# Weight sums of the feed-forward part planned one stage later, and lighter work around the first norm

## The chip, the cores and the metric

The kernel runs on one core of a Trainium2 chip. The metric is the device time of one execution in microseconds (us). The names of the engines are those of the profile: PE (matrix multiplication), PEld (its weight loads, which overlap it), DVE (vector), ACT (scalar), POOL (GpSimd) and SP, whose queue issues nearly all transfers (DMA). Every engine takes its instructions in the order in which they stand in its queue.

## The reference

One decoder layer is computed in float32 for 2048 prompt tokens and 64 sample tokens (8 sequences of 8) with shared weights, width 1024:

```python
hp = rmsnorm(xp, norm_mix_w[l])
mp, sr_p, sh_p = mixer(hp, pos_p, zero_ret, zero_hg, w_in[l], ...)
hs = rmsnorm(xs, norm_mix_w[l])
ms, sr_s, sh_s = mixer(hs, pos_s, state_ret[l], state_hgrn[l], w_in[l], ...)
xp = xp + mp
xs = xs + ms
hp = rmsnorm(xp, norm_ffn_w[l])
xp = xp + jnp.square(jax.nn.relu(hp @ w_up[l])) @ w_down[l]
hs = rmsnorm(xs, norm_ffn_w[l])
xs = xs + jnp.square(jax.nn.relu(hs @ w_up[l])) @ w_down[l]
```

The mixer projects to 4096 columns (`w_in`), runs four retention heads and four gated linear recurrences (HGRN2) over chunks, normalises each head, gates it, and projects back (`w_out`). The feed-forward part has 4096 inner columns. The outputs are the two normalised results and the final states of both recurrences.

## The kernel before

**Tiling and stages.** The tokens are cut in three groups: the first holds the 64 sample tokens and 512 of the prompt (576), the other two 768 prompt tokens each. The mixing part goes through them in turn: `mix` (four pairs of heads each) and then `out_proj`. In the profile `mix` of the first group lies at about 0 to 290 us, its `out_proj` up to 345, `mix` of the second group at 345 to 638, its `out_proj` up to 714, `mix` of the third group at 714 to 1010 and its `out_proj` up to 1076. Then come the three feed-forward stages, up to the end.

**A product.** A float32 product is made of three matmuls of rounded parts (high by high, high by low, low by high). So each weight block is loaded (`raw`), its high part cast on ACT (L310, into `hi`) and its low part subtracted on DVE (L318, into `lo`). Parts that were split before are loaded as they are (`hi<-fki0VA12hi`, `lo<-fki0VA12lo`). There are eight `raw` buffers and three `hi`/`lo` pairs. The two banks of `pj` take the products by turns, so a product that is two later than another has to wait until DVE has taken the earlier one out (L1035 and L1122 do that).

**Seven products for eight.** In the second and third group a pair of heads is computed with Strassen's scheme (Winograd's form) in two halves: a P part, seven products with L1848 (128x384 a matmul), and a V part, seven products with `product_t` (L1107, 128x256). Both take 84 ticks. The weights of four of the seven products are sums of weight blocks, named S1 to S4. For `w_in` these sums are made once, in the first group, by `in_sums` (DVE L417, stored by SP L424). For the feed-forward weights they are made ahead by `plan_sums`: a set has four loads of 512 KB (SP L1877), four sums on DVE (L1880, 128x1024) and four stores of 512 KB (SP L1885). There are 16 sets; a set's key is u0 to u7 or d00 to d31.

**What sets the order.** PE work counts ticks: `tick` is called after every two matmuls or so. `at` and `later` put a function on an agenda of ticks, `hold` puts one on a list of absolute ticks (`n_ticks`), and `plan_sums` has a queue of its own (`side`). A scheduler then puts each engine's instructions in an order; those inside `keep_in_program_order` stay as written.

**The first norm.** At the start `norm_in` rounds eight blocks of the input (ACT L715, DVE L716) while PE already multiplies them. The 64 sample columns of each high and low part are copied apart by POOL (L721, 16 copies, into `hs`). The squares (ACT L693) are added up on POOL and DVE by turns (L696), L774 adds the two halves, and PE sums the columns (L743). Two working buffers for the samples (`qm`) are cleared by POOL at L917. While the last heads of a group are computed, `norm_ahead` loads the next group's input a second time in eight quarters, squares each on ACT (L805) and adds it on DVE (L807).

**The last layers.** `out_proj` adds the residual on DVE (L246), and stores two results for the feed-forward part (`fres` and `fin`, SP L1912); `prepare` loads `fin` again (SP L1920).

Of the kernel before, what the change touches and what calls it, by code (L numbers as in the profile page):

```python
# [21 lines left out]
NS = NSEQ * SLEN  # L22
PAST = 16384
H = 4
# [28 lines left out]
NQ = FF // (4 * P)  # L53
# [152 lines left out]
class Kernel:  # L206
# [105 lines left out]
    def second_part(self, j):  # L312
        self.first_part(j)
        if j in self.second:
            hi, lo = self.wts[j]
            raw = self.second.pop(j)
            for c in (slice(0, WT),) if j else LEADS:
                self.nc.vector.tensor_tensor(out=lo[:, c], in0=raw[:, c], in1=hi.bitcast(F32)[:, c], op=ALU.subtract)  # L318
            if self.fast and j < N_IN:
                self.whole[j] = raw  # L320
                if j < 4:
                    if j >= 2:
                        self.hold((50, 74)[j - 2], self.in_sums, j)
                elif j % 4 >= 2:
                    self.in_sums(j)

# [166 lines left out]
    def build(self):  # L493
        nc, tc, I = self.nc, self.tc, self.I
        with ExitStack() as ctx:
# [84 lines left out]
            sums = [(("u", t), W_UQ0 + 4 * t) for t in range(NQ)]  # L580
# [2 lines left out]
            self.mix(gs[0])  # L583
            self.out_proj(gs[0], 1, lambda: norm(gs[1]))

            at = [84 * j if self.fast else 16 + 92 * j for j in range(2 * H)]
            self.plan_sums(sums[:NQ], at)
            self.mix(gs[1])
            self.out_proj(gs[1], 1, lambda: norm(gs[2]))
            self.plan_sums(sums[NQ:], at)  # L590
            self.mix(gs[2])

            def end_of_mixing():
# [105 lines left out]
    def norm_in(self, g, start=False, pace=5):  # L699


        nc, T = self.nc, g.T
        g.h, g.sq = [], None
        g.starts = ([0] if g.ns else []) + [g.ns + C * c for c in range(g.n // C)]

        def piece(kb):
            x, hi, lo = self.x_block(g, kb, start), self.getr(), self.getr()
            if start and kb == 0:
                raw = self.raws[0] = self.wp.tile([P, WT], F32, tag="raw", name="raw", bufs=self.n_raw)
                for c in LEADS:  # L710
                    self.fetch(raw[:, c], self.I["w"][0][:, c])
                self.ahead, self.w_load = 0, 1
                self.weight(0)
            w = self.vec[:, V_MIX + kb:V_MIX + kb + 1]
            nc.scalar.activation(hi[:, :T], x[:, :T], AF.Copy, scale=w)  # L715
            nc.vector.scalar_tensor_tensor(out=lo[:, :T], in0=x[:, :T], scalar=w, in1=hi.bitcast(F32)[:, :T],  # L716
                                           op0=ALU.mult, op1=ALU.subtract)
            if g.ns:

                for part, a in ((hi, 0), (lo, NS)):  # L720
                    nc.gpsimd.tensor_copy(self.hs[kb][:, a:a + NS], part[:, :NS])  # L721
            g.h.append((hi, lo))
            if start:
                g.x.append(x)
            else:
                g.sq = self.add_square(g, g.sq, x, nc.vector)

        def tables():
            cs = self.I["cs"].rearrange("p (a t) -> p a t", a=2)
            g.cos, g.sin = self.load(), self.load()  # L730
            self.fetch(g.cos[:, :T], cs[:, 0, g.off:g.off + T])
            self.fetch(g.sin[:, :T], cs[:, 1, g.off:g.off + T])

        def split():
            g.sq = self.halves(g, g.sq)

        def factor():
            g.rs, ln = self.get(), self.get()
            for hf, (c0, c1) in enumerate(g.pieces):
                sl = slice(c0, c1)  # L740
                ps = self.mm(c1 - c0)
                if start:
                    nc.tensor.matmul(ps, self.ones, g.sq[:, sl], start=True, stop=True)  # L743
                else:
                    self.column_sums(ps, *g.sq[hf])
                self.rsqrt(g.rs[:, sl], ps, ln[:, sl], self.eps, D)

        def factor_t():

            row = self.dp.tile([1, g.starts[-1] + C], F32, name=self.tag + f"r{g.i}")  # L750
            g.rt = self.small.tile([P, 8], F32, tag="rt", name="rt")
            nc.sync.dma_start(row, g.rs[0:1, :T])
            n0, m = g.ns, g.n // C
            with nc.allow_non_contiguous_dma("a column for each chunk"):
                nc.sync.dma_start(g.rt[:, len(g.starts) - m:len(g.starts)], row[0, n0:T].rearrange("(c p) -> p c", p=P))
                for a in range(0, P if n0 else 0, NS):
                    nc.sync.dma_start(g.rt[a:a + NS, 0:1], row[0, 0:NS].rearrange("(c p) -> p c", p=NS))

        def rotary():
            for t in (g.cos, g.sin):  # L760
                (nc.vector if self.fast else nc.gpsimd).tensor_tensor(out=t[:, :T], in0=t[:, :T], in1=g.rs[:, :T], op=ALU.mult)

        if start:
            g.x = []
            for kb in range(KB):
                piece(kb)
            part = [None, None]

            def square(kb):
                part[kb % 2] = self.add_square(g, part[kb % 2], g.x[kb], (nc.gpsimd, nc.vector)[kb % 2])  # L770

            def both():
                g.sq = part[0]
                nc.vector.tensor_tensor(out=g.sq[:, :T], in0=g.sq[:, :T], in1=part[1][:, :T], op=ALU.add)  # L774

            for kb in range(KB):
                self.at(24 + 2 * kb, square, kb)
            self.at(24 + 2 * KB, both)
        else:
            for kb in range(KB):  # L780
                self.later(pace * kb, piece, kb)
        t0 = 66 if start else pace * KB
        self.later(0 if start else t0, tables)
        if not start:
            self.later(t0 + 9, split)
        self.later(t0 + (0 if start else 20), factor)
        self.later(t0 + 24, rotary)
        self.later(t0 + 24, factor_t)

    def norm_ahead(self, g, early):  # L790


        nc, T, T2, n = self.nc, g.T, g.T // 2, g.n // C
# [37 lines left out]
            return  # L831
        todo = [(m, v, h) for h in range(2) for m in range(2) for v in range(2)]
        for k, a in enumerate(todo):
            self.later(1 + 9 * k, load, *a)
            self.later(12 + 9 * k, square, *a)
        for h in range(2):
            self.later(52 + 36 * h, split, h)
            self.later(60 + 36 * h, factor, h)
# [73 lines left out]
    def mix(self, g):  # L912
        nc = self.nc
        if g.ns:
            g.qm = [self.get(), self.get()]
            for q in g.qm:
                nc.gpsimd.memset(q, 0.0)  # L917
        g.o, g.oc = {}, {}
        end = 0
        for p in range(H):  # L920
# [1548 lines left out]
```

## Time and profile before

| What | Value |
|---|---|
| Median of 3 runs | 2384.07 us (2382.16 to 2389.36) |
| Profiled execution | 2385.9 us |
| Span in its profile | 2384.1 us |
| PE busy | 2353.4 us (99%) |
| DVE busy | 1800.1 us (76%) |
| ACT busy | 1229.9 us (52%) |
| POOL busy | 148.7 us (6%) |
| Data moved | 575.60 MB, 241 GB/s in the mean |

PE is busy for all but 30.7 us of the span. Each group of rows in the profile has a line, an engine, an operation, the tiles out<-in, a count and times; `PE pj L1107 <- DVE slab L1122` reads: PE's instruction of line 1107 that writes `pj` waited for what DVE wrote at line 1122. Rows of a time line start with the start time and the busy time of the group, and end with the idle time of the engine before it and what ended it. Rows by stretch give the stretch, its length, and the busy time and number of instructions of PE, PEld, DVE, ACT and POOL, then the TensorE clock that was granted (1.00 is full speed), the busy share of the DMA engines and GB/s.

### The profile page before, as it was taken

The numbers are of one execution on the slowest core, as the hardware profiler recorded it, in microseconds if no ns is written. First come the engines' busy times: TensorE is split into PE (matmuls) and PEld (weight loads), VectorE is DVE, ScalarE is ACT, GpSimd is POOL, SyncE is SP. The second block draws the span as 40 slices with busy tenths as digits, with TensorE's granted clock in tenths as the row PEclk, the third lists the DMA queues.
The fourth block names the chain that finished last, engine by engine and source line by source line (L and its number), as shares of the span: only waits on it lengthen the run. The fifth ranks groups of instructions, "written<-read, shape, count | busy, mean of one in ns | idle before, by whom it ended". The sixth has DMA issues, their size and how long they took to land.

```text
span 2384.1 us, 39317 instructions
## 1 busy us (share of the span) xinstructions
PE 2353.4 (99%) x15322; PEld 2313.5 (97%) x15322; DVE 1800.1 (76%) x2299; ACT 1229.9 (52%) x1974; POOL 148.7 (6%) x202
## 2 busy tenths in 40 slices
PE   9999999999999999999999999999999999999998
PEld 8888799999999999999999999999999999999997
DVE  7666777767676766757769997666998786669887
ACT  5555564466654555536555555444544364445444
POOL 4212201010001001000000000000000000000000
PEclk9999999999999999999999999999999999999999
DMA  8888788788858777968677665766755457575541
GB/s 284 288 295 285 253 282 311 280 287 288 315 199 308 289 285 267 322 218 294 227 244 268 234 214 183 241 212 223 243 185 191 152 188 262 201 237 178 203 152 71
DMA packets 232505, 575.60 MB, mean 241 GB/s; under 512 B 24179, under 2 KB 92659, under 8 KB 232310
## 3 DMA queue, kind: packets, MB, share of 16 engines
q1 hardware_dynamic: 232166, 572.98, 69.9%
q8 instruction: 122, 2.00, 0.3%
q14 instruction: 73, 0.60, 0.1%
q10 hardware_dynamic: 144, 0.02, 0.0%
HBM read 419.95 MB, written 151.66 MB: 240 GB/s over the span
## 4 chain that ended last, share of the span: by engine, by line
PE 81%; DVE 2%; DMA 1%; ACT 0%; issue 0%; POOL 0%; SPq 0%; DVEq 0%; ACTq 0%
PE pj L1848 34%; PE pf L1848 28%; PE pj L1107 9%; PE pj L452 6%; PE mm L1690 1%; PE mm L1688 1%; PE mm L1696 1%; PE mm L1618 0%; PE mm L1465 0%; PE mm L1376 0%; DMA lo<-fki0VA12lo 0%; PE mm L1837 0%; DMA raw<-w 0%; DMA fo<-slab 0%; DVE raw L1880 0%
## 5 line engine op out<-in xcount | busy, mean ns | idle before, releaser
L1848 PE MATMUL pj<-slab,hi 128*128 128x384 f32 (+1 forms) x3504 | 853.5, 326 | 1.4 <-ACT slab L1030 1.4
L310 ACT CAST hi<-raw 128x1024 fp32r<-128x1024 f32 (+1 forms) x449 | 470.6, 1049 | 676.0 <-PE pj L1848 258.9
L318 DVE TENSOR_TENSOR lo<-raw,hi 128x1024 fp32r<-128x1024 f32 (+1 forms) x449 | 551.8, 1229 | 165.9 <-ACT hi L310 147.1
L1848 PE MATMUL pf<-slab,hi 128*128 128x384 f32 (+1 forms) x2768 | 652.5, 321 | 0.0
L1848 PEld LDWEIGHTS pj<-slab,hi 128*128 128x128 f32 x3504 | 614.6, 188 | 1.7 <-ACT slab L1030 1.7
L1848 PE MATMUL pj<-slab,lo 128*128 128x384 f32 (+1 forms) x1752 | 570.6, 326 | 0.6 <-DVE lo L318 0.6
L1848 PEld LDWEIGHTS pf<-slab,hi 128*128 128x128 f32 x2768 | 480.6, 188 | 0.1
L1848 PE MATMUL pf<-slab,lo 128*128 128x384 f32 (+1 forms) x1384 | 443.1, 320 | 0.0
L1848 PEld LDWEIGHTS pj<-slab,lo 128*128 128x128 f32 x1752 | 329.3, 188 | 1.0 <-DVE lo L318 1.0
L1107 PE MATMUL pj<-hi,slab 128*128 128x256 f32 x1344 | 264.9, 290 | 6.9 <-DVE slab L1122 4.8
L452 PE MATMUL pj<-slab,hi 128*128 128x288 f32 (+1 forms) x1280 | 259.1, 318 | 2.0 <-ACT slab L715 1.1
L1848 PEld LDWEIGHTS pf<-slab,lo 128*128 128x128 f32 x1384 | 260.1, 188 | 0.0
L1107 PEld LDWEIGHTS pj<-hi,slab 128*128 128x128 f32 x1344 | 217.7, 193 | 8.3 <-ACT G L1439 5.1
L452 PEld LDWEIGHTS pj<-slab,hi 128*128 128x128 f32 x1280 | 206.5, 190 | 5.9 <-issue 1.9
L1107 PE MATMUL pj<-lo,slab 128*128 128x256 f32 x672 | 191.5, 285 | 0.8 <-DMA lo<-fki0VA12lo 0.8
L1940 ACT CAST slab<-slab 128x768 fp32r<-128x768 f32 (+1 forms) x192 | 145.5, 779 | 64.8 <-DVE slab L1951 47.3
L1944 DVE TENSOR_TENSOR slab<-slab 128x768 fp32r<-128x768 f32 (+1 forms) x192 | 167.3, 886 | 13.2 <-ACT slab L1940 4.6
L452 PE MATMUL pj<-slab,lo 128*128 128x288 f32 (+1 forms) x640 | 150.0, 315 | 0.0
L1107 PEld LDWEIGHTS pj<-lo,slab 128*128 128x128 f32 x672 | 130.1, 194 | 1.0 <-DMA lo<-fki0VA12lo 1.0
L452 PEld LDWEIGHTS pj<-slab,lo 128*128 128x128 f32 x640 | 108.6, 190 | 0.1
L2194 DVE TENSOR_TENSOR slab<-pf,slab 128x768 f32<-128x768 f32 (+1 forms) x87 | 76.5, 885 | 24.4 <-PE pf L1848 24.3
L2194 DVE TENSOR_TENSOR slab<-pj,slab 128x768 f32<-128x768 f32 (+1 forms) x79 | 70.1, 888 | 20.5 <-PE pj L1848 20.3
(269 smaller groups left out, 2614.4 us busy)
## 6 DMA issues: line engine op xcount, KB each, us to landing
raw<-w SPq DMA_DIRECT2D x255, 512.0 KB, 4.8
slab<-fu SPq DMA_DIRECT2D x64, 384.0 KB, 5.5
fu<-ld SPq DMA_DIRECT2D x60, 384.0 KB, 3.8
ld<-x SPq DMA_DIRECT2D x40, 384.0 KB, 5.5
ld<-fin SPq DMA_DIRECT2D x28, 384.0 KB, 4.8
slab<-fu SPq DMA_DIRECT2D x32, 288.0 KB, 4.5
fu<-ld SPq DMA_DIRECT2D x30, 288.0 KB, 3.2
fres<-slab SPq DMA_DIRECT2D x16, 384.0 KB, 4.6
```

Source lines behind the costliest of these rows:

```text
L310: self.nc.scalar.copy(self.wts[j][0][:, c], raw[:, c])
L318: self.nc.vector.tensor_tensor(out=lo[:, c], in0=raw[:, c], in1=hi.bitcast(F32)[:, c], op=ALU.subtract)
L452: self.nc.tensor.matmul(pj[:, i, :T2], w, a[:, c0:c1], start=j == 0 and q == 0, stop=j == n - 1 and q == 2)
L1107: self.nc.tensor.matmul(ps[:, tb * 256:(tb + 1) * 256], t, w[:, cols], start=first and kb == j == 0 and tb != 1, stop=kb == KB // 2 - 1 an ...
L1688: nc.tensor.matmul(dst, am(c), b["vc"][c][hd], start=True, stop=first)
L1690: nc.tensor.matmul(dst, qd[:, cols[c]], S, start=False, stop=True)
L1696: nc.tensor.matmul(ps[:, hd * P:(hd + 1) * P], kt[:, c * P:(c + 1) * P], b["vc"][c][hd], start=True, stop=True)
L1848: self.nc.tensor.matmul(*a, **k)
L1940: self.nc.scalar.copy(hi[:, :g.T], B[name][:, :g.T])
L1944: self.nc.vector.tensor_tensor(out=lo[:, :g.T], in0=B[name][:, :g.T], in1=hi.bitcast(F32)[:, :g.T], op=ALU.subtract)
L2194: nc.vector.tensor_tensor(out=r, in0=ps, in1=r, op=ALU.add)
```

## The change

Five places are edited, all on the path taken here (`self.fast`).

1. The sums of the first two weight pairs of `w_in` (`in_sums(2)`, `in_sums(3)`) are held until tick 78 and 94 instead of 50 and 74.
2. Each set of feed-forward sums starts 84 ticks later, which is one half of a pair of heads: the first P part of the second and of the third group has none. The second group makes seven sets instead of eight and the third nine, of which the last two start at tick 672 and 740 of the third group. Its `mix` has 8 x 84 = 672 ticks, so these two run in its `out_proj`.
3. The 16 copies of the sample columns are put on the agenda at tick 48 and on, one block a tick, instead of right behind each block.
4. `norm_ahead` loads and adds its quarters every 7 ticks instead of every 9: the last load at tick 50 instead of 64, the last square at 61 instead of 75.
5. The two clearings of `qm` are put at tick 60.

```diff
-                        self.hold((50, 74)[j - 2], self.in_sums, j)
+                        self.hold((78, 94)[j - 2], self.in_sums, j)
...
-            at = [84 * j if self.fast else 16 + 92 * j for j in range(2 * H)]
-            self.plan_sums(sums[:NQ], at)
+            at = [84 * j + 84 if self.fast else 16 + 92 * j for j in range(2 * H)]
+            m = NQ - 1 if self.fast else NQ
+            self.plan_sums(sums[:m], at)
...
-            self.plan_sums(sums[NQ:], at)
+            self.plan_sums(sums[m:], at + [740])
...
-                for part, a in ((hi, 0), (lo, NS)):
-                    nc.gpsimd.tensor_copy(self.hs[kb][:, a:a + NS], part[:, :NS])
+                def rows(kb=kb, hi=hi, lo=lo):
+                    for part, a in ((hi, 0), (lo, NS)):
+                        nc.gpsimd.tensor_copy(self.hs[kb][:, a:a + NS], part[:, :NS])
+                self.at(48 + kb, rows) if start and self.fast else rows()
...
-            self.later(1 + 9 * k, load, *a)
-            self.later(12 + 9 * k, square, *a)
+            self.later(1 + 7 * k, load, *a)
+            self.later(12 + 7 * k, square, *a)
...
-                nc.gpsimd.memset(q, 0.0)
+                self.at(60, nc.gpsimd.memset, q, 0.0) if self.fast else nc.gpsimd.memset(q, 0.0)
```

The changed kernel's own lines are 1 later from L588 on and 3 later behind L721, so its L697, L777, L1038, L1110 and L1125 are L696, L774, L1035, L1107 and L1122 of before.

Below is what stands in the queues at three places. DVE at the first norm, before (L774 is the add for which PE's L743 waits):

```order
L417 TENSOR_TENSOR raw<-raw 128x512
L696 TENSOR_TENSOR slab<-slab 128x576
L417 TENSOR_TENSOR raw<-raw 128x512
L696 TENSOR_TENSOR slab<-slab 128x576
L417 TENSOR_TENSOR raw<-raw 128x512
L696 TENSOR_TENSOR slab<-slab 128x576
L417 TENSOR_TENSOR raw<-raw 128x512
L318 TENSOR_TENSOR lo<-raw,hi 128x1024
L774 TENSOR_TENSOR slab<-slab 128x576
```

and the same place of DVE in the changed kernel:

```order
L697 TENSOR_TENSOR slab<-slab 128x576
L417 TENSOR_TENSOR raw<-raw 128x512
L697 TENSOR_TENSOR slab<-slab 128x576
L417 TENSOR_TENSOR raw<-raw 128x512
L697 TENSOR_TENSOR slab<-slab 128x576
L417 TENSOR_TENSOR raw<-raw 128x512
L777 TENSOR_TENSOR slab<-slab 128x576
L417 TENSOR_TENSOR raw<-raw 128x512
L318 TENSOR_TENSOR lo<-raw,hi 128x1024
```

One sum of weights and the L318 of the fourth weight block have moved behind the add.

PE in the V part of the first pair of heads of the second group, where the third product ends and the fourth begins, before. What stands in square brackets is what a matmul waits for (DMAHW are transfers, Activation is ACT):

```order
L1107 MATMUL pj<-lo,slab 128x256
L1107 MATMUL pj<-hi,slab 128x256
L1107 MATMUL pj<-hi,slab 128x256 [waits DMAHW2_49,Activation_49]
L1107 MATMUL pj<-hi,slab 128x256 [waits DVE_49,Activation_49]
L1107 MATMUL pj<-lo,slab 128x256
L1107 MATMUL pj<-hi,slab 128x256 x2
L1107 MATMUL pj<-lo,slab 128x256
L1107 MATMUL pj<-hi,slab 128x256
L1107 MATMUL pj<-lo,slab 128x256 [waits DMAHW3_49]
```

and there in the changed kernel:

```order
L1110 MATMUL pj<-lo,slab 128x256
L1110 MATMUL pj<-hi,slab 128x256
L1110 MATMUL pj<-hi,slab 128x256 [waits DMAHW7_49,Activation_49]
L1110 MATMUL pj<-lo,slab 128x256 [waits DMAHW0_49]
L1110 MATMUL pj<-hi,slab 128x256 x2
L1110 MATMUL pj<-lo,slab 128x256
```

The matmul that waits for DVE and ACT stood between the first high and the first low part of the new product, and has moved 24 rows (a whole product of 36 matmuls) back.

DVE in the second group's last pair of heads, from the end of the P part into the V part, before (L807 adds squares of the third group's norm, L1880 is a feed-forward weight sum, L1035 takes a product out of its bank):

```order
L1735 SCALAR_TENSOR_TENSOR slab<-mm,ss,slab 128x128 x4
L807 TENSOR_TENSOR slab<-slab 128x768
L1035 TENSOR_TENSOR slab<-pj,slab 128x768
L1880 TENSOR_TENSOR raw<-raw 128x1024
L1059 TENSOR_TENSOR slab<-slab,ld 128x768
L807 TENSOR_TENSOR slab<-slab 128x768
L1060 TENSOR_TENSOR slab<-slab,ld 128x768
L1035 TENSOR_TENSOR slab<-pj,slab 128x768
L1064 TENSOR_TENSOR slab<-slab 128x384 x2
L1880 TENSOR_TENSOR raw<-raw 128x1024
L318 TENSOR_TENSOR lo<-raw,hi 128x1024
L807 TENSOR_TENSOR slab<-slab 128x768
```

and the same place of DVE in the changed kernel:

```order
L810 TENSOR_TENSOR slab<-slab 128x768
L1738 SCALAR_TENSOR_TENSOR slab<-mm,ss,slab 128x128 x4
L1038 TENSOR_TENSOR slab<-pj,slab 128x768
L810 TENSOR_TENSOR slab<-slab 128x768
L1883 TENSOR_TENSOR raw<-raw 128x1024
L1062 TENSOR_TENSOR slab<-slab,ld 128x768
L1063 TENSOR_TENSOR slab<-slab,ld 128x768
L1038 TENSOR_TENSOR slab<-pj,slab 128x768
L1067 TENSOR_TENSOR slab<-slab 128x384 x2
L1883 TENSOR_TENSOR raw<-raw 128x1024
L318 TENSOR_TENSOR lo<-raw,hi 128x1024
L1062 TENSOR_TENSOR slab<-slab,ld 128x768
```

Of the three adds of squares before, two have moved ahead of L1880 and one out of this piece.

## The prediction

> **What bounds the kernel now.** I read the engines' shares first, then the waits of PE, then each wait's place in the time line.
>
> ```profile
> PE 2353.4 (99%) x15322; PEld 2313.5 (97%) x15322; DVE 1800.1 (76%) x2299; ACT 1229.9 (52%) x1974; POOL 148.7 (6%) x202
> ```
>
> ```profile
> PE pj L1107 <- DVE slab L1122: 4.8, 2, 4.0
> PE mm L743 <- DVE slab L774: 1.8, 1, 1.8
> PE pj L1107 <- DVE slab L1035: 1.8, 1, 1.8
> PE pj L1848 <- ACT slab L1030: 1.4, 1, 1.4
> ...
> PE pj L1107 <- DMA lo<-fki0VA12lo: 0.8, 1, 0.8
> PE pj L1848 <- DVE lo L318: 0.6, 1, 0.6
> ```
>
> PE is the bound. The change touches no matmul, so it can win only PE's idle time, 2384.1 - 2353.4 = 30.7 us, and the time in which PE runs at a lower clock; it can lose by new idle time. In the rows of waits (total us, times, longest) the largest are mostly single events. Their places:
>
> ```profile
> 29.18 1.82 PE L743 MATMUL mm<-slab,ones 128*128 128x288 f32 x4 [1.79 <-DVE slab L774]
> ...
> 388.20 0.55 PE L1107 MATMUL pj<-hi,slab 128*128 128x256 f32 x1 [4.00 <-DVE slab L1122]
> ...
> 602.47 0.36 PE L1107 MATMUL pj<-hi,slab 128*128 128x256 f32 x1 [1.79 <-DVE slab L1035]
> ```
>
> All three are followed by slow matmuls. The stretches (PE's busy us and matmuls stand third, the granted clock third from the end):
>
> ```profile
> 28.00:31.00 3.00, 1.82 (x5) 1.37 (x6) 2.93 (x5) 0.89 (x2) 0.00 (x0) 0.78 0.97 303
> 31.00:34.00 3.00, 3.00 (x17) 3.00 (x17) 2.97 (x5) 1.35 (x4) 0.00 (x0) 0.65 0.54 190
> ...
> 387.00:390.00 3.00, 1.80 (x8) 1.83 (x9) 2.29 (x3) 2.44 (x5) 0.45 (x2) 0.68 0.03 12
> 390.00:393.00 3.00, 3.00 (x22) 3.00 (x21) 2.49 (x3) 0.47 (x1) 0.00 (x0) 0.75 0.00 0
> ...
> 603.00:606.00 3.00, 3.00 (x17) 3.00 (x16) 2.83 (x5) 2.21 (x4) 0.00 (x0) 0.52 1.04 414
> 606.00:609.00 3.00, 3.00 (x25) 2.99 (x25) 3.00 (x6) 1.93 (x4) 2.17 (x2) 0.91 0.75 302
> ...
> 723.00:726.00 3.00, 1.65 (x9) 1.66 (x10) 1.23 (x1) 1.29 (x2) 0.00 (x0) 1.00 1.04 423
> ```
>
> Busy time times (1 - clock) is what the clock costs: 1.82 x 0.22 + 3 x 0.35 = 1.45 us after the first stall, 1.80 x 0.32 + 3 x 0.25 = 1.33 after the second, 3 x 0.48 + 3 x 0.09 = 1.71 after the third. After the 1.4 us wait for L1030 (the stretch from 723) the clock stayed at 1.00. So a stall of 1.8 us costs about 3.3, one of 1.4 us its own length. The Trainium skill (TensorE: Matmul & The Clock Gate, What's actually happening) has the clock halve after an idle window of about 3.4 us that runs freely. By that rule the first and third stall would have cost no clock and the sum below would be 1.7 + 0.7 us smaller; the granted clock of 0.52 behind a stall of 1.79 us decides against it.
>
> **The sums one stage later, at the second group's start.** Set u0 leaves the P part at 345 to 374. What DVE does there:
>
> ```profile
> 362.96 1.40 DVE L1880 TENSOR_TENSOR raw<-raw 128x1024 f32<-128x1024 f32 x1
> 364.28 2.86 DVE L318 TENSOR_TENSOR lo<-raw,hi 128x1024 fp32r<-128x1024 f32 x1
> ...
> 375.08 1.22 DVE L1880 TENSOR_TENSOR raw<-raw 128x1024 f32<-128x1024 f32 x1
> ...
> 387.11 0.95 DVE L1122 TENSOR_TENSOR slab<-pj,slab 128x768 f32<-128x768 f32 x1
> ```
>
> The L318 at 364.28 is the one for which PE waits 0.6 us; with the L1880 of 1.40 gone from ahead of it that wait goes: -0.6 (bounds -0.6 and 0).
>
> The 4.0 us wait at 388.20 has another cause. PE's order shows it: a matmul that needs DVE's L1122 stands between the first high and the first low part of the product ahead of its own, so 36 matmuls that need nothing of DVE are stuck behind it. In the changed order it follows them. The row to size this is the stretch 393 to 396:
>
> ```profile
> 393.00:396.00 3.00, 3.00 (x28) 3.00 (x27) 0.47 (x1) 1.16 (x3) 0.00 (x0) 1.00 0.09 15
> ```
>
> 28 matmuls take 3.0 us, so 36 take about 3.9. PE ran dry at 388.20 - 4.00 = 384.20 and would ask for L1122 at 388.1 instead, 387.5 with the earlier 0.6 us. L1122 ended at 387.11 + 0.95 = 388.06; with the L1880 at 375.08 (1.22 us) out of DVE's unbroken run, and the same 0.6, it ends at 386.2. That is 1.3 us of slack: the whole stall goes with its clock, -4.0 - 1.3 = -5.3. Bounds: -5.3, and 0 if the matmuls that now come first wait for their own low part instead.
>
> **At the third group's start** the set that leaves takes its transfers along: 4 loads and 4 stores of 0.52 MB are 4.2 MB.
>
> ```profile
> 744.00:756.00 12.00, 11.18 (x89) 10.81 (x88) 12.00 (x19) 7.70 (x9) 2.90 (x3) 1.00 1.03 418
> ```
>
> At 418 GB/s this is 10 us of a DMA that is full here, and the 0.8 us wait for `lo<-fki0VA12lo` falls in this stretch: -0.8 (bounds -0.8 and 0). The wait of 1.4 us for ACT's L1030 at 724 stands behind an L310 in both orders: 0 (bounds -1.4 and 0).
>
> **Squares closer together.** At 602.47 PE waits for L1035, the end of an unbroken run of DVE that holds two L807:
>
> ```profile
> 592.08 0.96 DVE L1059 TENSOR_TENSOR slab<-slab,ld 128x768 f32<-128x768 f32 x1 [0.62 <-ACT slab L1056]
> 592.96 0.96 DVE L807 TENSOR_TENSOR slab<-slab 128x768 f32<-128x768 f32 x1
> ...
> 598.77 0.95 DVE L807 TENSOR_TENSOR slab<-slab 128x768 f32<-128x768 f32 x1
> ...
> 601.38 0.95 DVE L1035 TENSOR_TENSOR slab<-pj,slab 128x768 f32<-128x768 f32 x1
> ```
>
> One of them moves out of the run (0.88 us, the step from the first row to the second) and one into the idle 0.62 us ahead of it, so L1035 comes 0.88 + 0.62 = 1.5 earlier. A stall of 0.3 us is left, as short as others here that cost no clock: -1.5 - 1.7 = -3.2. Bounds: -3.5, and 0 if the eight loads of 384 KB, now within 49 ticks instead of 63, make another transfer late there (the DMA stands at 1.04).
>
> **The start.** L774 has two instructions fewer ahead of it:
>
> ```profile
> 22.87 1.91 DVE L417 TENSOR_TENSOR raw<-raw 128x512 f32<-128x512 f32 x1
> ...
> 25.37 0.68 DVE L417 TENSOR_TENSOR raw<-raw 128x512 f32<-128x512 f32 x1
> ...
> 27.25 1.21 DVE L318 TENSOR_TENSOR lo<-raw,hi 128x1024 fp32r<-128x1024 f32 x1
> 28.38 0.74 DVE L774 TENSOR_TENSOR slab<-slab 128x576 f32<-128x576 f32 x1
> ```
>
> That is 1.13 for L318 (up to the next row) and 0.68 for an L417, together 1.8. But POOL now makes its copies at that very time:
>
> ```profile
> 9.09 6.54 POOL L721 CAST slab<-slab 128x64 fp32r<-128x64 f32 x12 [0.68 <-DVE slab L716]
> 15.57 1.41 POOL L917 MEMSET slab<- 128x768 f32 x2
> ...
> 19.05 5.18 POOL L696 TENSOR_TENSOR slab<-slab 128x576 f32<-128x576 f32 x3 [1.88 <-ACT slab L693]
> ```
>
> Beside POOL's adds an L417 took 1.91, behind them 0.68. Sixteen copies of up to 0.55 us (12 in 6.54) lie behind those adds now. Five DVE instructions up to L774, each held up by some 0.2 (between nothing and a copy's 0.55), give 1.0 us back, and two copies ahead of POOL's third add a little more. The Trainium skill (SBUF — State Buffer, Who interferes with whom) states that a DVE instruction with two SBUF inputs and a GpSimd one that reads SBUF exclude each other for a whole instruction; the 1.91 agrees. By that rule each could lose a full copy, 5 x 0.55 = 2.7, and the term would be 0. I take -0.7 for the stall and half of the 1.45 of clock: -1.4. Bounds: -3.2, and +1.5 if the L318 behind L774 comes late for the next weight block. The clearings (1.41 us) hide in POOL's idle time, 94% of the span.
>
> **The two sets in the last `out_proj`.** 8.4 MB and eight L1880 (1.22 each, 9.8 us of DVE) move into 1010 to 1076.
>
> ```profile
> 1010.00:1076.00 66.00, 66.00 (x406) 65.97 (x405) 33.31 (x56) 25.07 (x57) 0.60 (x3) 1.00 0.69 233
> 1076.00:1100.00 24.00, 24.00 (x182) 24.00 (x181) 18.65 (x22) 17.18 (x24) 0.00 (x0) 1.00 0.85 304
> ```
>
> DVE has 33 us free. DMA has 31% of 66 us, 20.5 us, and the sets need 8.4 MB at 418 GB/s, 20.1. What is hidden is hidden just so. SP also stands in line: each store waits for its L1880, with residual loads behind it, and loads of feed-forward weights that used to go out early now go out behind the results' stores:
>
> ```profile
> 1044.86 0.32 SPq L252 DMA_DIRECT2D raw<-fsu0S  x1
> 1053.18 0.33 SPq L252 DMA_DIRECT2D raw<-fsu0S  x1
> ...
> 1061.63 0.33 SPq L252 DMA_DIRECT2D raw<-fsu0S  x1
> ...
> 1078.48 0.53 SPq L252 DMA_DIRECT2D raw<-w  x1
> ```
>
> Three loads come 17 to 34 us later. PE uses a block of 24 matmuls at 24/182 us each in about 3.2 us there, and about six blocks are in hand at 1078 (three loaded, three split), so I expect a short stall at most: +0.5 (bounds 0 and +18, below). The first group's matmuls change order too, and its small waits move: +0.7 (bounds -1.5 and +2).
>
> **Sum.** -0.6 - 5.3 - 0.8 - 3.2 - 1.4 + 0.5 + 0.7 = -10.1 against the profiled execution's 2385.9, which gives 2375.8. That execution is 1.8 us above the median of 2384.07, so a median of 2374.0 is forecast, 0.42% faster. 0.3%, 7.2 us, is about what a measurement of this kernel can tell from no change.
>
> **Rivals.**
> - *The waits move on.* DVE stays as busy; what comes off one wait shows at the next product. Against it: DVE is busy only 0.47 of the 3 us behind 393 and the slack worked out is 1.3 us; for it: these slacks are short. With half of the 8.5 us of the two large terms kept, -0.6 - 0.8 - 1.4 - 4.25 + 1.2 = -5.85, so 2378.2: the same.
> - *The squares' loads find a full DMA* and the 3.2 us stay lost. For it: DMA share 1.04 at 603; against: these loads end earlier. 2374.0 + 3.2 = 2377.2: the same.
> - *The last `out_proj` starves the feed-forward part* (slower). SP stands in order, so only half of its free DMA time can be used; 10 us of transfers spill over 1076, where the share is 0.85. PE runs out of weights about five times for 2 us, and each stall of that length costs 1.6 us of clock: +18, so 2374.0 + 18 = 2392. It decides from 17.3 us on (7.2 + 10.1); with less the result is "the same". Against it: PE shows no idle time there now, and weights are loaded several blocks ahead.
>
> **How the numbers follow.** 0.62 for the forecast and its neighbours above 0.3%; 0.20 for the moving waits and 0.08 for the squares, both within 0.3%; 0.10 for the starved feed-forward part. The forecast's own range is 2369.5 (1.4 for L1030, 1.8 more at the start, 1.3 of the two plus terms) to 2376.9. The whole range goes to 2385, which takes in both middle cases and a starvation of up to 11 us.
>
> **What would show it.** Right: the waits for L1122, L1035 and `lo<-fki0VA12lo` gone or below 0.5 us, the granted clock at 1.00 in 387 to 393 and 603 to 609, PE idle about 20 us in the span, and no idle time between 1010 and 1110. Wrong: a wait of PE for `raw`, L310 or L318 behind 1076, a wait for L318 or L774 near 30 that is as long as before, or a new wait for L1122 or a low part near 384.

## The result, and the profile after

| Kernel | Median | Kernel before, same chip | Ratio, 95% interval |
|---|---|---|---|
| changed (15 runs) | 2381.15 us | 2384.81 us | 0.9981 [0.9974, 0.9989] |
| changed, measured again (7 runs) | 2378.83 us | 2384.84 us | 0.9971 [0.9959, 0.9982] |

The change makes the kernel 0.2 to 0.3% faster, 3.7 us in the first measurement and 6.0 in the second; the forecast was 10.1. The two intervals overlap between 0.9974 and 0.9982, which is 4.3 to 6.2 us; why the medians differ was not found. The profiled execution took 2380.17 us, its span 2378.4. It lies 1.0 us under its median and the profiled execution of before 1.1 us above its own, so the profiles show a larger gain (5.7 us) than the first pair of medians.

The shares of the engines and the waits of PE in the changed kernel:

```profile
PE 2349.0 (99%) x15322; PEld 2308.3 (97%) x15322; DVE 1794.9 (75%) x2299; ACT 1230.1 (52%) x1974; POOL 156.6 (7%) x202
```

```profile
PE pj L1194 <- ACT slab L1205: 2.1, 2, 1.8
PE pj L1190 <- ACT slab L474: 1.4, 1, 1.4
PE pj L1851 <- ACT slab L1033: 1.4, 1, 1.4
PE pj L1194 <- DVE slab L1005: 1.4, 3, 0.8
PE pj L1190 <- DVE slab L1005: 1.2, 1, 1.2
PE pj L1110 <- DVE slab L1125: 1.1, 2, 0.8
...
PE mm L677 <- DVE slab L671: 1.0, 1, 1.0
...
PE pj L1110 <- DVE slab L1038: 0.7, 1, 0.7
...
PE mm L746 <- DVE slab L777: 0.3, 1, 0.3
```

The three waits behind which the clock fell are gone or short (L1122 is now L1125, L774 is L777, L1035 is L1038), and so are those for `lo<-fki0VA12lo` and L318. In their place stand new ones of 0.7 to 1.8 us, most of them in the first group. PE's idle time went from 30.7 to 2378.4 - 2349.0 = 29.4 us, hardly at all: 1.3 of the 5.7 us between the two spans. The rest is PE's busy time, down from 2353.4 to 2349.0 with the same 15322 matmuls, and that is the clock: before, it was at one half for 3.41 us behind each of the three stalls of the prediction, which is up to 1.7 us of PE's time each. In the changed kernel it stood at full speed in all the stretches in which it was low before (the matmuls of the last one run 6 us earlier by now, and the clock stood at full speed there too):

```profile
28.00:31.00 3.00, 3.00 (x25) 3.00 (x24) 2.90 (x5) 2.55 (x5) 3.00 (x6) 1.00 0.42 117
387.00:390.00 3.00, 3.00 (x27) 3.00 (x26) 2.14 (x3) 2.43 (x5) 0.46 (x3) 1.00 0.65 195
390.00:393.00 3.00, 3.00 (x27) 3.00 (x26) 2.42 (x3) 1.57 (x4) 0.00 (x0) 1.00 0.87 324
...
600.00:603.00 3.00, 3.00 (x27) 2.93 (x26) 2.82 (x7) 2.97 (x6) 1.36 (x2) 1.00 1.03 419
```

Where the time went is read best from PE itself. The table gives, for every kernel that was profiled, how much later the matmul of the same number in PE's order starts than in the kernel before, in us; the columns are times in the kernel before. Negative is ahead. A step between two columns is what that part of the program won or lost. e9 is the changed kernel again; the others are told below.

| Profile | 45 | 345 | 400 | 560 | 640 | 660 | 760 | 1076 | 2300 |
|---|---|---|---|---|---|---|---|---|---|
| changed | -2.0 | +1.4 | -5.2 | -5.2 | -5.9 | -4.8 | -6.0 | -6.0 | -6.0 |
| e9, changed again | -1.3 | +0.9 | -5.7 | -5.8 | -6.4 | -5.5 | -6.8 | -6.8 | -6.8 |
| e1, sums and squares | +0.9 | +1.2 | -5.4 | -5.4 | -6.0 | -4.9 | -6.2 | -6.2 | -6.2 |
| e2, sums | -0.9 | -1.7 | -8.3 | -8.3 | -8.3 | -7.1 | -8.4 | -8.4 | -8.4 |
| e3, holds | -1.7 | +0.4 | +1.4 | +1.4 | +0.6 | +0.6 | +0.7 | +0.7 | +0.7 |
| e4, copies | -0.1 | -0.7 | +0.5 | +0.5 | -0.3 | +0.3 | -0.1 | -0.1 | -0.1 |
| e5, order of PE | +0.5 | +0.7 | -5.0 | -5.0 | -1.4 | -0.8 | -1.1 | -1.1 | -1.1 |
| e6, sums and order | -1.5 | -1.9 | -8.4 | -8.4 | -4.2 | -3.5 | -5.7 | -5.7 | -5.7 |
| e7, sums, squares by 8 | -1.4 | -1.8 | -8.4 | -8.4 | -9.5 | -8.2 | -9.5 | -9.5 | -9.5 |
| e8, sums, squares by 6 | -1.4 | -0.3 | -6.9 | -6.9 | -8.3 | -7.0 | -8.4 | -8.4 | -8.4 |
| e10, all but the holds | -0.2 | -0.3 | -6.9 | -6.9 | -7.5 | -6.9 | -8.2 | -8.2 | -8.2 |
| e11, e10 with squares by 8 | +0.3 | +1.1 | -5.5 | -5.5 | -6.7 | -5.7 | -7.0 | -7.1 | -7.1 |

The column of 45 us is to be read with care: e1, e2, e5, e6, e7 and e8 have the start of the kernel before and lie between -1.5 and +0.9 there. So much is chance of one execution. From 400 to 640 us the steps repeat to within 0.1 us among kernels with the same spacing of the squares, apart from what the clock does and from the pins of e5 and e6.

### The profile page after: what moved, and what is told of

It reads as the page before. It is cut to its first block, busy times and chain, and to the rows that moved or that the text cites. A ratio compares the mean times of both kernels' runs of the same rounds, so it can differ in the third digit from the quotient of the medians.

```text
span 2378.4 us, 39303 instructions
## 1 busy us (share of the span) xinstructions
PE 2349.0 (99%) x15322; PEld 2308.3 (97%) x15322; DVE 1794.9 (75%) x2299; ACT 1230.1 (52%) x1974; POOL 156.6 (7%) x202
## 4 chain that ended last, share of the span: by engine, by line
PE 86%; DVE 1%; DMA 1%; ACT 1%; POOL 0%; issue 0%; SPq 0%; DVEq 0%; ACTq 0%
PE pj L1851 36%; PE pf L1851 28%; PE pj L1110 9%; PE pj L452 7%; PE mm L1691 1%; PE mm L1693 1%; PE mm L1699 1%; PE mm L1840 1%; PE mm L1468 0%; PE mm L1621 0%; PE mm L1379 0%; DMA ld<-fo 0%; PE pj L1194 0%; DMA ld<-x 0%; DVE slab L1423 0%
## 5 line engine op out<-in xcount | busy, mean ns | idle before, releaser
L310 ACT CAST hi<-raw 128x1024 fp32r<-128x1024 f32 (+1 forms) x449 | 470.6, 1048 | 688.0 <-PE pj L1851 267.2
L318 DVE TENSOR_TENSOR lo<-raw,hi 128x1024 fp32r<-128x1024 f32 (+1 forms) x449 | 547.9, 1220 | 169.9 <-ACT hi L310 165.5
L1110 PE MATMUL pj<-hi,slab 128*128 128x256 f32 x1344 | 261.7, 287 | 2.0 <-DVE slab L1125 1.1
L1110 PEld LDWEIGHTS pj<-hi,slab 128*128 128x128 f32 x1344 | 215.3, 191 | 3.3 <-ACT slab L1441 1.0
L1110 PE MATMUL pj<-lo,slab 128*128 128x256 f32 x672 | 190.0, 283 | 0.0
L1110 PEld LDWEIGHTS pj<-lo,slab 128*128 128x128 f32 x672 | 128.7, 192 | 0.0
```

Source lines behind the costliest of these rows:

```text
L310: self.nc.scalar.copy(self.wts[j][0][:, c], raw[:, c])
L1110: self.nc.tensor.matmul(ps[:, tb * 256:(tb + 1) * 256], t, w[:, cols], start=first and kb == j == 0 and tb != 1, stop=kb == KB // 2 - 1 an ...
```

## The experiments

The theory after the first profile (A in the expectations): the shift of the sums wins about what was forecast for it, the changed kernel gives back in the first group what it saves at the start, and the closer squares trade one wait for others. The rivals: the sums' own loads disturb the first group; the wait at 388 us was made by DVE's load and not by PE's order.

**The sums and the squares without the start (e1), and the sums alone (e2).** e1 is the changed kernel with the holds, copies and clearings as before; e2 has only this of the change:

```diff
-            at = [84 * j if self.fast else 16 + 92 * j for j in range(2 * H)]
-            self.plan_sums(sums[:NQ], at)
+            at = [84 * j + 84 if self.fast else 16 + 92 * j for j in range(2 * H)]
+            m = NQ - 1 if self.fast else NQ
+            self.plan_sums(sums[:m], at)
...
-            self.plan_sums(sums[NQ:], at)
+            self.plan_sums(sums[m:], at + [740])
```

> The changed kernel without its three edits at the start (holds of the first weight sums, sample copies and clearings are as before). Theory A, that the changed kernel gives back at waits of the first group what it saves at the start, and wins only behind 345 us: PE stands within 0.3 us of the kernel before up to 345, is 6.5 to 8 us ahead at 780, and the median is 2376 to 2379, 2 to 4 us better than the changed kernel. Rival B, that the sums' shift and its earlier loads cause the new waits of the first group: those waits (1.8 us for L1205 at 131, 1.2 for L1005 at 243) are here too, and the median is 2381 to 2383.

> Only the feed-forward sums one stage later. Theory A: the wait of 4.0 us for L1122 at 388 is gone, with the slow clock behind it and the 0.6 us for L318 (together 6 to 7 us), and the 0.8 us for fki0VA12lo at 755; the wait of 1.8 us for L1035 at 602 stays, with slow clock where it falls in one window; median 2377 to 2380. Rival: the 4.0 us come back in the same stage and the median is within 2 us of the kernel before.

Measured: e1 2378.79 us, ratio 0.9967 [0.9955, 0.998]; e2 2377.73 us, 0.9964 [0.9949, 0.9978]. In e1 the wait for ACT at 131 us was 0.5 instead of 1.8 and that for L1005 at 243 was 0.5 instead of 1.2, so the sums do not cause them. PE stood 0.6 to 1.2 us behind from 45 to 345, more than the 0.3 I had expected, and 0.9 of it is there at 45 already, as the chance of the start; so it is 6.2 us ahead at 780 and not 6.5 to 8. The median is in the expected range and 2.4 us under the changed kernel's first one, but level with its second. In e2 the wait at 388 is gone and the one for L1035 is there, with its clock:

```profile
594.17 0.36 PE L1108 MATMUL pj<-hi,slab 128*128 128x256 f32 x1 [1.79 <-DVE slab L1036]
```

The sums alone are worth all that the whole change is worth: their ratio is the lower one, though its interval overlaps with both of the changed kernel's. From 345 to 400 every kernel that has them gained 6.5 to 6.6 us.

**The start in two parts: the holds (e3) and the copies with the clearings (e4),** each alone on the kernel before.

> Only the first weight sums held longer. Theory A: the wait for L774 near 29 us is under 0.5 us, PE is 2 to 3.5 us ahead at 35 us, but under 1 us ahead at 140 and at 345, since the waits for DVE's rotary products near 37 and for a transfer at 131 take it back; median within 1.5 us of before. Rival: holding the sums is itself what costs the first group time (their stores and the loads of the next sums come late), and PE is behind the kernel before by 1 us or more at 345.

> Only the sample copies and the clearings moved behind the first norm. Theory A: POOL runs without a break from 17 to 37 us, its L1003 (free to start near 34) comes 1 to 3 us late, and PE is 0 to 2.5 us behind the kernel before at 60; median 0 to 2.5 us above before. Rival: copies off POOL ahead of the first squares speed up the start, and PE is 1 us or more ahead at 60 and at 345.

e3: 2386.44 us, ratio 1.0004 [0.9995, 1.0014]. e4: 2386.05 us, 1.0000 [0.9991, 1.0010]. Neither gives a difference that the medians can tell. They also showed that I had put the cause of one thing in the wrong place. It is the copies that put L774 earlier in DVE's order and cut its wait: 0.34 us in e4, but still 1.37 in e3, where I had expected under 0.5 (in the other kernels without the moved copies it is 1.17 to 1.80). And the holds cost the first group 2.1 us between 45 and 345 in e3: PE was 3.3 us ahead at 35, as expected, but still 1.4 at 140 (under 1 expected) and 0.4 behind at 345, between theory A and its rival.

In e4 what L774 gives is taken back 12 us later. POOL in e4, then PE there:

```profile
24.43 10.85 POOL L722 CAST slab<-slab 128x64 fp32r<-128x64 f32 x14
35.22 1.41 POOL L225 MEMSET slab<- 128x768 f32 x2
36.60 2.06 POOL L1005 TENSOR_TENSOR slab<-slab,ld 128x576 f32<-128x576 f32 x1
```

```profile
38.20 0.47 PE L1189 MATMUL pj<-hi,slab 128*128 128x512 f32 x1 [2.47 <-DVE slab L1004]
```

and DVE ahead of it:

```profile
36.16 1.23 DVE L318 TENSOR_TENSOR lo<-raw,hi 128x1024 fp32r<-128x1024 f32 x1 [0.98 <-ACT hi L310]
37.30 0.75 DVE L1004 TENSOR_TENSOR slab<-pj,ld 128x576 f32<-128x576 f32 x1
```

The 14 copies take 0.78 us each beside DVE (12 took 6.54 us, 0.55 each, before), so POOL comes to L1005, the L1003 of before at 34.99, 1.6 us late, as expected. PE's new wait, though, is not for POOL but for DVE's L1004 (L1002 of before). DVE's queue from L774 on holds the sums, two L318 and the rotary products, and the L318 just ahead had waited 0.98 us for ACT's cast: PE was 4.3 us ahead there, DVE only 0.7. Between 35 and 45 us (of the kernel before) PE's lead falls by 4.2 us in e4 (from 4.3 to 0.1) and in e10 (from 4.4 to 0.2), in the changed kernel by 2.6 (from 4.6 to 2.0). About 1.6 us of that is no fault of the copies: it falls by so much in all six kernels that have the start of before, and in e3. Another 1.7 in e4 and e10 is the clock, which fell to one half for 3.4 us behind this stall of 2.5 us; in the changed kernel PE waits 1.4 us there, and the clock stays up. PE stood 0.1 us ahead at 60 in e4, at the edge of what I had expected (0 to 2.5 behind).

**The changed kernel again, and without the holds (e9, e10, e11).** e10 has this edit on the changed kernel, and e11 besides it the squares every 8 ticks:

```diff
-                        self.hold((78, 94)[j - 2], self.in_sums, j)
+                        self.hold((50, 74)[j - 2], self.in_sums, j)
```

> The changed kernel once more, beside the two below on the same chip. If the 6.0 us by which its first profile stood ahead of the kernel before were partly chance of the clock's windows at the start, this profile stands less far ahead at 20 us (0 to -1.5) and the same 3 us are lost again between 45 and 345; ratio 0.997 to 0.999.

> The changed kernel with the holds of the first weight sums put back to 50 and 74. Theory A, that the holds cost the first group 2 to 3 us (waits for L1205 at 131, L1333 at 206, L1005 at 243): those waits are as before, PE loses under 1 us between 45 and 345, and the median is 1.5 to 3 us under the changed kernel's. Rival B, that the loss comes with whatever makes PE earlier at the start: it loses 2 us or more there too and the medians are within 1 us of each other.

> The same with the squares every 8 ticks. Theory A: 1 to 2 us under the one with 7 at 615, since the wait for L671 near 584 is 0.3 us instead of 1.0; the lowest median of all, 8 to 10 us under the kernel before. Rival: the two paces differ by less than 0.5 us.

e9: 2378.83 us, 0.9971 [0.9959, 0.9982]; e10: 2378.00 us, 0.9969 [0.9958, 0.9980]; e11: 2378.35 us, 0.9969 [0.9957, 0.9981]. The changed kernel lost 2.1 us again between 45 and 345 (3.3 in its first profile); without the holds it lost 0.0, and the wait for ACT at 131 us was 0.79 us instead of 1.95. Over this stretch the three profiles with the holds moved (changed, e9, e3) lose 2.1 to 3.3 us; the nine others with the holds of before lie between 0.8 us won and 1.2 lost, e11 at 0.8 lost (and e8's 1.2 has 1.7 us of half clock in it). So the holds make most of the first group's loss. But they help at the start: with the copies moved and without the holds (e4, e10, e11) PE waits 2.5 us for DVE near 38 us and the clock falls behind it, with both (changed, e9) it waits 1.4 and the clock stays, and PE is 1.0 to 2.2 us further ahead at 45. In the trace this is theory A, in the medians rival B: 0.8 us is left, less than the 1.5 to 3 expected, and the intervals do not tell e9, e10 and e11 apart. That e11 would have the lowest median of all did not come true either: it stood 0.8 us behind e10 at 615, not 1 to 2 ahead. What the squares by 8 win over those by 7 between 400 and 640 is there (1.2 us against 0.6); the rest it had lost in the first group.

How a hold of sums ends as a wait for ACT is seen at 131 us. ACT before, after, and in e9:

```profile
129.26 1.05 ACT L310 CAST hi<-raw 128x1024 fp32r<-128x1024 f32 x1 [6.67 <-DMA fki1VA22hi<-hi]
130.21 0.37 ACT L1378 COPY slab<-mm 128x256 f32<-128x256 f32 x1
130.48 0.85 ACT L1202 ACTIVATE slab<-pj,rt 128x256 f32<-128x256 f32 x2
```

```profile
129.06 1.04 ACT L310 CAST hi<-raw 128x1024 fp32r<-128x1024 f32 x1 [4.84 <-DMA fki1VA22hi<-hi]
130.01 0.36 ACT L1381 COPY slab<-mm 128x256 f32<-128x256 f32 x1
130.28 0.84 ACT L1205 ACTIVATE slab<-pj,rt 128x256 f32<-128x256 f32 x2
```

```profile
129.90 1.04 ACT L310 CAST hi<-raw 128x1024 fp32r<-128x1024 f32 x1 [4.74 <-DMA fki1VA22hi<-hi]
```

The L310 waits for a store that frees its buffer, and L1202, for which PE waits, stands behind it. In the changed kernel PE is 1.3 us ahead at 125, but this store and so the L310 come only 0.2 us earlier: what PE had gained it waits here. In e9, 0.6 us ahead at 125, the L310 comes 0.6 us later than before. In e7, which has the holds of before and is 1.4 us ahead there, it comes 1.5 us earlier (127.78), and PE loses nothing. That the stores of the first weight sums, which the hold moves among these transfers, keep the store late was not tried by itself.

**The cause of the 4.0 us at 388 (e5), and the same cure for the wait at 724 (e6).** e5 is the kernel before with its sums where they were, and the first matmul of each product of the V parts pinned behind the matmuls written ahead of it; e6 pins the products of both parts, on top of the sums' shift.

```diff
-                    self.nc.tensor.matmul(ps[:, tb * 256:(tb + 1) * 256], t, w[:, cols], start=first and kb == j == 0 and tb != 1,
-                                          stop=kb == KB // 2 - 1 and j == 2, skip_group_check=True)
+                    mm = self.nc.tensor.matmul(ps[:, tb * 256:(tb + 1) * 256], t, w[:, cols], start=first and kb == j == 0 and tb != 1,
+                                               stop=kb == KB // 2 - 1 and j == 2, skip_group_check=True)
+                    if tb == kb == j == 0:
+                        self.tc.keep_in_program_order(mm)
```

> The kernel before, its sums and paces untouched; only the first matmul of each product of the V parts is kept behind the matmuls written ahead of it, so that the one that waits for L1122 follows the product it stood in. Theory A, that the 4.0 us wait at 388 is made by PE's order: the wait falls to under 0.8 us although all of DVE's sums are still there, PE is 4.5 to 7.5 us ahead at 400, median 4 to 7 us under before. Rival B, that DVE's load makes it: L1122 is as late as before and PE waits 3 us or more, at the new place; median within 1.5 us of before.

> The sums one stage later, and the first matmul of each product of both P and V parts kept in its written order. If the order explains the wait for L1030 (1.1 to 1.4 us near 717 to 724) as it explains the one at 388, that wait falls under 0.4 us, the rest stands as with the sums alone, and the median is 0 to 2 us under that of the sums alone (2377.7). If the pins hold up other matmuls, new waits show behind 570 and the median is above it.

e5: 2384.70 us, 0.9996 [0.9986, 1.0006]; e6: 2381.08 us, 0.9982 [0.9973, 0.9992]. In e5 the wait at 388 is gone although every sum is still in DVE's queue: L1122 (here L1124) ends no earlier than before,

```profile
386.62 1.22 DVE L318 TENSOR_TENSOR lo<-raw,hi 128x1024 fp32r<-128x1024 f32 x1
387.75 0.95 DVE L1124 TENSOR_TENSOR slab<-pj,slab 128x768 f32<-128x768 f32 x1
```

at 388.7 (388.1 before, where PE stood 0.7 us earlier), and PE gains 5.7 us from 345 to 400 and stands 5.0 ahead at 400, as theory A had it. That is rival B's end: the order of PE made that stall, with its clock. The 6.6 us of the sums are this and the 0.6 us for L318, with 0.3 besides. The median is only 0.4 us under before, not 4 to 7: what spoiled e5 is the pin itself. It pulled the sums of the next norm (L675) ahead of the product in the last V part, long before they were ready:

```profile
600.90 0.69 PE L675 MATMUL mm<-slab,ones_r 128*128 128x384 f32 x1 [5.21 <-ACT slab L669]
```

e6 has the same new wait of 5.2 us, which costs it more than the pins bring (its median is 3.4 us above that of the sums alone, where 0 to 2 under was one of the two outcomes foreseen); the wait for L1030 near 720 did go there (0.6 us for a transfer is left).

**The squares every 8 and every 6 ticks (e7, e8),** with the sums' shift and nothing else:

```diff
-            self.later(1 + 9 * k, load, *a)
-            self.later(12 + 9 * k, square, *a)
+            self.later(1 + 8 * k, load, *a)
+            self.later(12 + 8 * k, square, *a)
```

> The sums one stage later, and the next norm's squares every 8 ticks. Theory A, that closer squares shorten the wait for L1035 near 594 but bring the half sums' L671 and the loads ahead of ACT's casts in the way: the wait for L1035 is between 0.5 and 1.8 us, a wait for L671 of 0 to 1 us appears near 575, median within 1 us of the sums alone. Rival: the step of 8 has the gain without the new wait, PE is 1.5 us or more ahead of the sums alone at 615.

> The same with the squares every 6 ticks. Theory A: the wait for L1035 is under 0.8 us, the one for L671 or another for DVE near 575 to 590 is 1 us or more, median within 1.5 us of the sums alone. Rival: all squares are done before the V part, both waits are gone, PE is 1.5 us or more ahead of the sums alone at 615.

e7: 2376.78 us, 0.9963 [0.9949, 0.9977]; e8: 2376.87 us, 0.9962 [0.9950, 0.9975], like the sums alone (0.9964). As theory A had it, the wait for L1035 shortens or goes and others come: in e7 0.33 us for L671 and 1.09 for an L310 of ACT, in e8 0.97 for L671 and 0.22 for L1035. e7 stood 1.8 us ahead of the sums alone at 615, which is what its rival had asked for; that is mostly the clock, which fell in e2 behind the 1.79 us and not in e7, and by 640 1.2 us of it is left. Between 400 and 640 the squares every 9 ticks win 0.8 us where the clock stays up (e3, e4) and nothing where it falls (before, e2), those every 7 win 0.6 (changed, e1, e9, e10), every 8 1.2 (e7, e11) and every 6 1.4 (e8). The medians of e2, e7 and e8 are lower than the changed kernel's in either measurement, e7's by 2.1 us under the second one; they were not run beside it on one chip, and the intervals of the ratios overlap, so this is not shown to be a difference.

## Why the prediction was right or wrong

| Step of the forecast | Forecast | Changed | e9 |
|---|---|---|---|
| start and first group's other waits (-1.4 and +0.7) | -0.7 | +1.4 | +0.9 |
| u0 out of the second group's start (-0.6 and -5.3) | -5.9 | -6.6 | -6.6 |
| squares closer together | -3.2 | -0.6 | -0.6 |
| (not foreseen) at 645 us | 0 | +1.0 | +0.9 |
| third group's start | -0.8 | -1.2 | -1.3 |
| the two sets in the last `out_proj` | +0.5 | 0.0 | 0.0 |
| sum | -10.1 | -6.0 | -6.8 |

The 4.1 us between the sums are the squares (2.6), the start (2.1) and 645 us (1.0), less 1.6 by which the other three steps beat the forecast. The sign that was to show the forecast right, PE idle for about 20 us, did not come: 29.4 us are left.

**Right: the sums' shift.** The wait at 388 us was read from PE's order, and e5 shows that reading: the order alone removes it. The end of L1122 was mis-sized. In the changed kernel, where L1125 is L1122 and L1062 is L1059 of before:

```profile
380.70 0.96 DVE L1062 TENSOR_TENSOR slab<-slab,ld 128x768 f32<-128x768 f32 x1 [1.22 <-ACT slab L1059]
...
386.96 0.95 DVE L1125 TENSOR_TENSOR slab<-pj,slab 128x768 f32<-128x768 f32 x1
```

It ended at 387.9 where PE stood 1.4 us later than in the kernel before, which is 386.5 on the forecast's scale and not 386.2, since DVE stood idle for 1.22 us where I had taken its run as unbroken; the slack was about 1.0 us instead of 1.3 and still enough. The wait for `lo<-fki0VA12lo` went with the transfers, and the one for L1030 stayed, as said.

**Right: the two sets in the last `out_proj` cost nothing.** No step of the table between 760 and 2300 is above 0.1 us, although the DMA there filled up:

```profile
1010.00:1076.00 66.00, 66.00 (x410) 65.97 (x409) 44.54 (x61) 26.51 (x48) 0.40 (x2) 1.00 0.92 329
```

Its share rose from 0.69 to 0.92, DVE's time from 33 to 45 us, and PE was busy throughout. The rival of a starved feed-forward part did not come.

**Wrong: the squares (-3.2).** The step said that L1035 would come 1.5 us earlier, leave 0.3 us and cost nothing else. It left 0.7, and two others came:

```profile
584.10 0.44 PE L677 MATMUL mm<-slab,ones_r 128*128 128x384 f32 x1 [0.98 <-DVE slab L671]
...
597.38 0.35 PE L1110 MATMUL pj<-hi,slab 128*128 128x256 f32 x1 [0.73 <-DVE slab L1038]
...
609.69 0.39 PE L1110 MATMUL pj<-hi,slab 128*128 128x256 f32 x1 [0.26 <-DVE slab L1125]
```

Together 1.97 us of idle time, where e4 with the old spacing has 1.79 and 0.25. So the 1.5 us of idle time were not saved at all. The 1.7 us of clock were mis-sized as well: e3 and e4 have the old spacing and the same stall, the clock happened to stay up behind it, and they won only 0.8 us on the kernel before between 400 and 640, since part of what PE gains there it waits for L1122 at 615 (0.25 us). The changed kernel's 0.6 is no more than that. I had followed the adds of squares that left L1035's queue and not where they went. DVE ahead of L671, which PE's norm sums wait for, in the changed kernel:

```profile
577.91 1.41 DVE L318 TENSOR_TENSOR lo<-raw,hi 128x1024 fp32r<-128x1024 f32 x1 [2.41 <-ACT hi L310]
580.22 0.96 DVE L1038 TENSOR_TENSOR slab<-pj,slab 128x768 f32<-128x768 f32 x1 [0.90 <-POOL slab L1051]
581.10 0.95 DVE L810 TENSOR_TENSOR slab<-slab 128x768 f32<-128x768 f32 x1
...
582.36 1.22 DVE L1883 TENSOR_TENSOR raw<-raw 128x1024 f32<-128x1024 f32 x1
583.50 0.55 DVE L671 TENSOR_TENSOR slab<-slab 128x384 fp32r<-128x384 f32 x1
```

In the kernel before these L318, L1035 and L670 start at 583.15, 584.62 and 587.01, and PE is 5.2 us ahead of it here. So the L318 comes on time, L1038 0.8 us late, behind the 0.90 us for POOL, and L671 1.7 us late, since one add of squares (L810) now stands between. In e7 there is the add but no wait for POOL, and PE's wait for L671 is 0.33 us instead of 0.98. Why POOL is late there was not tried.

**Wrong: the start (-1.4 and +0.7).** That L774 would come earlier held, and more than forecast: its wait went to 0.3 us and in e9 under 0.25, since the copies hardly slowed DVE (an L417 beside them took 0.72 us). But the forecast gave this gain a place in the sum without asking what PE does next. PE comes to the rotary products 4.6 us ahead of the kernel before at 35 us (e9: 3.9) and is 2.0 ahead at 45 (e9: 1.3), 2.6 lost in both, 1.6 of which every other profile loses there too. Nor was the clock behind L774 worth anything: e1 and e5 have the stall of 1.80 us without the half clock, and they stand at 45 us where they stood at 20 (0.9 and 0.5 us behind before); what a clock at full speed gives them up to 35 us they wait near 38 to 43. So the changed kernel won 0.5 us between 20 and 45 (e9: 0.7). Then the holds cost 2 to 3 us up to 345. In the forecast "the first group's matmuls change order too" stood for this with a range of -1.5 to +2, without a wait being followed. It is the first rival, the waits that move on: at the squares, where I had put it, and at the start, where I had not. At u0, the larger of the two terms that it named, it did not come.

**Not foreseen: 645 us.** In the second group's `out_proj` PE waits for ACT's L1448, 0.8 us in the changed kernel and 1.0 in e2, where it did not wait before: an ACT scaling ahead of it waits for a load of `x`, 2.5 us in the changed kernel and in e2 2.7 where it was 1.2 before:

```profile
640.95 1.12 ACT L861 ACTIVATE ld<-ld,vec 128x384 f32<-128x384 f32 x2 [2.68 <-DMA ld<-x]
```

Why that load lands later was not tried. The sums' shift cannot be all of it: e4 and e5, which do not have it, lose 0.6 and 0.7 us in these columns.

## What to carry to other kernels

Where an engine that is the bound waits, look first at what stands behind the waiting instruction in its own queue: the 4.0 us at 388 were 36 ready matmuls behind one that was not, and putting the order right won 5.7 us at that place with all of the other engine's work still there. A gain at a wait counts only up to the next point at which the other engines are ready; follow the same queue on to there, and do the same for each instruction that an edit moves to an earlier place. Time at a lower clock is no fixed price either: what PE loses in it can be time that it would have spent waiting a few us later. An edit that moves several things at once is worth taking apart: one of the five here made the whole gain; the others are worth nothing that the medians can tell, and in the traces the holds won 1 to 2 us at the start and lost 2 to 3 after it.

## What the runs showed of the hardware

Whether a stall of PE is followed by a slower clock differs between executions. The forecast took the 1.7 us of slow clock behind the stall at 602 as its fixed companion. In e4 the same stall of 1.79 us fell at 601.17 to 602.96, and the clock stayed up. The kernel before (shown in the prediction) had 0.52 in this stretch, e4 has:

```profile
600.00:603.00 3.00, 1.21 (x11) 1.04 (x10) 3.00 (x5) 1.04 (x1) 0.00 (x0) 1.00 1.02 416
603.00:606.00 3.00, 3.00 (x25) 3.00 (x26) 3.00 (x5) 1.72 (x3) 0.00 (x0) 1.00 1.04 411
```

Between the first 15 us and the idle end of the 13 profiles, each fall of the granted clock went to one half and lasted 3.4 or 6.8 us; four profiles have none. Of the nine stalls of PE from 1.76 to 1.95 us three were followed by one, of the 24 from 1.05 to 1.45 us none, and of the eight from 2.47 to 5.2 us all. The stall of 4.0 us was followed by 3.4 us of half clock in the kernel before and by 6.8 in e3 and e4:

```profile
387.00:390.00 3.00, 1.38 (x6) 1.41 (x7) 2.32 (x3) 2.02 (x4) 0.87 (x2) 0.56 0.25 100
390.00:393.00 3.00, 3.00 (x16) 3.00 (x15) 2.46 (x4) 0.89 (x2) 0.00 (x0) 0.50 0.00 0
```

(these two rows are e3's). The Trainium skill (TensorE: Matmul & The Clock Gate, What's actually happening) has windows of 3413 ns that run freely, and the lengths agree with that: within each profile the changes of clock lie a whole number of 3.41 us apart. But it asks for a whole idle window, and here stalls of 1.79 us, about half of one, were enough three times. Where the stall lies in its window does not decide it alone. Counted in steps of 3.41 us from the changes of clock of the same profile, those three lay inside one window; so did the two of 1.80 us in e1 and e5, and there the clock stayed up:

```profile
30.09 1.24 PE L744 MATMUL mm<-slab,ones 128*128 128x288 f32 x4 [1.80 <-DVE slab L775]
```

(e1's). And in e8 it fell at 255.7, for 3.4 us, behind two waits of 0.6 us with eight small matmuls around them:

```profile
253.70 0.64 PE L1838 MATMUL mm<-con,ld 64*128 64x64 f32 x3 [0.58 <-DMA ld<-fo]
254.93 1.14 PE L1838 MATMUL mm<-con,ld 128*128 128x128 f32 x5 [0.59 <-DMA ld<-fo]
```

```profile
255.00:258.00 3.00, 3.00 (x10) 2.29 (x11) 2.49 (x5) 2.27 (x4) 0.00 (x0) 0.61 1.07 337
```

What decides it stays open. Nor is 1.7 us what 3.4 us of half clock cost in the end: it was nothing at 29.7 (e1 and e5 against before), 0.8 us at 603 (e3 and e4 against before) and 1.7 at 388, where the gain of e5 is the stall of 4.0 us and 1.7 more. The spread of the kernel before (2382.16 to 2389.36) may come in part from this, which is not shown.
